# Two weight matrices turned token-major, the residual kept by rows, and the group at each stage boundary run once per half of the tokens

## The chip, the cores and the metric

The kernel runs on one core of one Trainium2 chip. The metric is the device time of one execution in microseconds (us), as the median over several runs. The kernel before takes 2888.52 us (3 runs, 2887.72 to 2889.67).

## The reference

The program computes one step of a two-layer backbone (`DEPTH = 2`) on 256 tokens: 128 context tokens (half 0) and 128 latent tokens (half 1), each half with its own modulation vector. The model width is 2048 and the FFN's hidden width is 8192. Everything is float32. What matters here of each layer:

```python
def _layer(x, cvec, p, attend):
    shift1, scale1, gate1, shift2, scale2, gate2 = _modulation(cvec, p['w_mod'], p['b_mod'])
    h = _rmsnorm(x, p['g_pre_mix']) * (1 + scale1) + shift1
    ...                                    # gMLP and attention branches on h @ w_in
    x = x + gate1 * _rmsnorm(merged @ p['w_out'], p['g_post_mix'])
    h = _rmsnorm(x, p['g_pre_ffn']) * (1 + scale2) + shift2
    f = jnp.square(jax.nn.relu(h @ p['w_ff1'])) @ p['w_ff2']
    x = x + gate2 * _rmsnorm(f, p['g_post_ffn'])
```

So each layer has two stages, mixing and FFN, and between two stages stands a chain that no matmul of the next stage can pass: the sum of squares of the last product over its whole row, the gated residual, the sum of squares of the new residual, and the modulated input `h` of the next stage. There are three such boundaries and an end.

## The kernel before, in words

All weights stream from HBM in tiles of 512 KB, 256 rows by 512 columns. One tile is one **job** (`Job`), and 4 or 8 jobs with the same 512 output columns are one **group** (`Group`, accumulated in PSUM over 8 jobs). The exact float32 product is made from three products of float32r halves: `split` (line 325) makes a high half `wh` on ScalarE (ACT) and a low half `wl` on VectorE (DVE) of every tile, and `mm_half` (line 333) issues the matmuls of one job. There are 928 jobs.

`mm_half` has two forms. With `tok=True` (lines 347 to 349, token-major) the activations are stationary and the weights move: 12 matmuls of 512 columns for a job, and the output has tokens on the partitions. Otherwise (lines 356 to 358, feature-major) the weights are stationary and the 256 tokens move: 24 matmuls of 256 columns for a job, and the output has features on the partitions. `w_out` (64 jobs in both layers), `w_ff1` and `w_ff2` (256 jobs each) are feature-major here, and so is the residual `X`.

The order of all engines' work is the program's order (`tc.manual_schedule`): a list `items` of jobs and callables is walked once. Before each item `advance` issues what it may: a load of a modulation tile while fewer than `MOD_BUFS` (4) are outstanding, a load of a weight tile while fewer than `RAW_BUFS` (6) are, and a split while fewer than `SPLIT_BUFS` (4) split tiles are unused. All loads go out on SP's queue in that order.

The modulation `m = silu(c) @ w_mod` is 384 further tiles ("mods", `one_mod`), in 48 quads of 8. A mod is done on TensorE (PE, `mod_mm`, line 241, for quads in `PE_QUADS`) or on DVE (`mod_dot`, two SCALAR_TENSOR_TENSOR of 1024 elements). Mods are mixed into the stream of jobs: one is issued after a job if a quota (`pace`) asks for it and a count of DVE's cost (`load["dve"]`, written up by each instruction and written down by 2.62 with each job) is below `MOD_LIMIT` (2.0). What must be there at a point is forced by `need(n)`, which issues all mods up to quad n at once. `ENDS` says which quad must be done at the end of each stage: 18, 30, 42, 48.

At a boundary (`boundary`, line 760) the steps are `s1` (root of the mean square, spread over the tokens by PE), `s2_` (residual and its squares, summed by 16 fp32 matmuls of `ones_sum`, line 260, for the two halves' tokens at once), `s3` (second root, first parts of `h`), and then single jobs of the next stage alternate with parts of `h_steps`. `FILLS` puts mods between these steps: quads 18, 19, 30, 31, 42 and 43 are PE mods for that reason. Their loads use up to `X_BUFS` (6) more buffers than the four. At the end, `s1` and `s2_` run alone and send `yT`.

## Time and profile before

| | |
|---|---|
| median of 3 runs | 2888.52 us |
| the profiled execution's own time | 2883.49 us |
| its span, first to last instruction | 2881.7 us |
| mean granted TensorE clock | 0.993 |
| PE busy / DVE busy / ACT busy | 98% / 72% / 46% |
| DMA | 714.63 MB, 248 GB/s mean |

The profile is one execution; its own time stands 5.0 us below the median of the runs. A busy PE is not PE at its peak, since the ends of matmuls are modelled and overlap: what tells PE's pace is the distance between the starts of its instructions. The stages lie at about 0 to 692 us (mixing 0), 717 to 1460 (FFN 0), 1483 to 2099 (mixing 1) and 2122 to 2863 (FFN 1).

### The profile page before, as it was taken

How to read it: one execution, taken by the hardware profiler on the slowest of the kernel's cores; microseconds unless marked ns; L12 is line 12 of the kernel's file. 1: busy time of each engine (PE TensorE's matmuls, PEld its weight loads, DVE VectorE, ACT ScalarE, POOL GpSimd, SP SyncE). 2: the span in 40 equal slices, each digit the busy share in tenths (PEclk: the TensorE clock that was granted, in tenths of full speed). 3: DMA queues.
4: the chain of work that ended last, by engine and by line, in shares of the span. 5: the costliest groups of instructions: out<-in, count | busy, mean ns of one | idle time of the engine just before them, and what ended most of it. 6: DMA issues, size and time to landing. Idle time of an engine off the chain costs nothing.

```text
span 2881.7 us, 50046 instructions
## 1 busy us (share of the span) xinstructions
PE 2821.7 (98%) x20552; PEld 2601.6 (90%) x20552; DVE 2075.3 (72%) x2647; ACT 1336.9 (46%) x1667; POOL 0.7 (0%) x6
## 2 busy tenths in 40 slices
PE   7999999999999999999989999999999999999997
PEld 5788778897999999999969987888979999999997
DVE  4665888888688777777666888898876556556555
ACT  4344554444544434434554445544554444353443
POOL 0000000000000000000000000000000000000000
PEclk9999999999999999999999999999999999999999
DMA  9978877789577777777776687787975566656653
GB/s 358 378 261 306 290 238 252 264 292 338 185 235 262 244 253 238 254 244 246 250 265 237 225 281 249 236 271 264 335 252 191 197 206 207 208 199 217 202 183 108
DMA packets 199046, 714.63 MB, mean 248 GB/s; under 512 B 22304, under 2 KB 24864, under 8 KB 198816
## 3 DMA queue, kind: packets, MB, share of 16 engines
q1 hardware_dynamic: 198816, 711.43, 71.6%
q8 instruction: 161, 2.64, 0.4%
q14 instruction: 69, 0.57, 0.1%
HBM read 705.04 MB, written 6.31 MB: 247 GB/s over the span
## 4 chain that ended last, share of the span: by engine, by line
PE 93%; DVE 3%; ACT 2%; issue 1%; DMA 1%; SPq 0%; ACTq 0%; DVEq 0%
PE mm L356 22%; PE mm L358 22%; PE mm L357 22%; PE mm L347 7%; PE mm L348 7%; PE mm L349 7%; PE aux L241 2%; DVE u L82 2%; PE aux L260 1%; ACT u L82 1%; DVE wl L82 1%; ACT wh L82 1%; DMA mraw<-wm 0%; DVE junk L82 0%; PE aux L545 0%
## 5 line engine op out<-in xcount | busy, mean ns | idle before, releaser
L82 DVE TENSOR_TENSOR wl<-raw,wh 128x1024 fp32r<-128x1024 f32 x928 | 1124.3, 1223 | 573.2 <-ACT wh L82 566.9
L82 ACT ACTIVATE wh<-raw 128x1024 fp32r<-128x1024 f32 x928 | 974.0, 1058 | 1212.3 <-PE mm L357 854.4
L356 PE MATMUL mm<-u,wh 128*128 128x256 f32 x5376 | 1525.2, 284 | 3.4 <-ACT wh L82 3.4
L358 PE MATMUL mm<-u,wl 128*128 128x256 f32 x5376 | 1522.1, 283 | 1.5 <-DVE wl L82 1.5
L357 PE MATMUL mm<-u,wh 128*128 128x256 f32 x5376 | 1522.8, 283 | 0.3
L356 PEld LDWEIGHTS mm<-u,wh 128*128 128x128 f32 x5376 | 1032.5, 192 | 18.2 <-issue 10.9
L358 PEld LDWEIGHTS mm<-u,wl 128*128 128x128 f32 x5376 | 1032.6, 192 | 1.9 <-DVE wl L82 1.9
L357 PEld LDWEIGHTS mm<-u,wh 128*128 128x128 f32 x5376 | 1032.6, 192 | 1.6 <-DVE u L82 1.1
L347 PE MATMUL mm<-wh,u 128*128 128x512 f32 x1024 | 407.0, 397 | 5.1 <-ACT u L82 2.7
L348 PE MATMUL mm<-wl,u 128*128 128x512 f32 x1024 | 400.2, 391 | 0.8 <-DVE wl L82 0.8
L349 PE MATMUL mm<-wh,u 128*128 128x512 f32 x1024 | 400.2, 391 | 0.2 <-DVE u L82 0.2
L82 DVE SCALAR_TENSOR_TENSOR mraw<-mraw,sbc 128x1024 f32<-128x1024 f32 x222 | 272.0, 1225 | 7.7
L82 DVE SCALAR_TENSOR_TENSOR junk<-mraw,sbc 128x1024 bf16<-128x1024 f32 x222 | 270.4, 1218 | 0.0
L347 PEld LDWEIGHTS mm<-wh,u 128*128 128x128 f32 x1024 | 192.9, 188 | 57.4 <-issue 12.8
L349 PEld LDWEIGHTS mm<-wh,u 128*128 128x128 f32 x1024 | 192.9, 188 | 42.4 <-DVE u L82 1.3
L348 PEld LDWEIGHTS mm<-wl,u 128*128 128x128 f32 x1024 | 193.2, 189 | 39.0 <-DVE wl L82 1.1
L82 DVE TENSOR_TENSOR u<-u,u 128x512 fp32r<-128x512 f32 (+3 forms) x139 | 104.2, 769 | 98.0 <-ACT u L82 97.2
L82 ACT ACTIVATE u<-u 128x512 fp32r<-128x512 f32 (+3 forms) x174 | 126.4, 746 | 72.5 <-DVE u L82 65.6
L82 ACT ACTIVATE u<-mm 128x1024 f32<-128x1024 f32 (+1 forms) x95 | 86.7, 925 | 146.5 <-PE mm L358 108.6
L82 DVE TENSOR_TENSOR u<-u,mm 128x1024 f32<-128x1024 f32 (+1 forms) x54 | 63.5, 1180 | 62.3 <-PE mm L358 50.8
L241 PE MATMUL aux<-mraw,csw 128*32 128x512 f32 (+1 forms) x332 | 47.9, 614 | 12.5 <-DMA mraw<-wm 12.4
L82 ACT ACTIVATE u<-u,mv 128x128 f32<-128x128 f32 x114 | 41.5, 431 | 16.1 <-DVE u L82 14.1
(93 smaller groups left out, 723.5 us busy)
## 6 DMA issues: line engine op xcount, KB each, us to landing
raw<-f SPq DMA_DIRECT2D x512, 512.0 KB, 4.3
mraw<-wm SPq DMA_DIRECT2D x297, 512.0 KB, 4.4
raw<-wi SPq DMA_DIRECT2D x288, 512.0 KB, 4.6
u<-wm SPq DMA_DIRECT2D x87, 512.0 KB, 9.3
raw<-wo SPq DMA_DIRECT2D x64, 512.0 KB, 5.0
raw<-pa SPq DMA_DIRECT2D x32, 512.0 KB, 4.7
raw<-pb SPq DMA_DIRECT2D x32, 512.0 KB, 4.4
u<-xT SPq DMA_DIRECT2D x8, 512.0 KB, 7.5
```

What stands on the lines that cost most here:

```text
L82: return fn(out, *a, **k)
L241: nc.tensor.matmul(p[32 * c:32 * c + 32, :128 * nb], csw[:, kt, :], r[:, kt - k0, :], start=kt < 4, stop=kt > 11, skip_group_check=True, t ...
L260: nc.tensor.matmul(o[:, :T], ones, t[:, b, :], start=first and b == 0, stop=last and b == n - 1)
L347: nc.tensor.matmul(o, hh, wh[:, j, :], start=first, stop=False)
L348: nc.tensor.matmul(o, hh, wl[:, j, :], start=False, stop=False)
L349: nc.tensor.matmul(o, lo, wh[:, j, :], start=False, stop=last)
L356: nc.tensor.matmul(o, wh[:, j, s], hh, start=first and b % 2 == 0, stop=False, **kw)
L357: nc.tensor.matmul(o, wh[:, j, s], lo, start=False, stop=False, **kw)
L358: nc.tensor.matmul(o, wl[:, j, s], hh, start=False, stop=last, **kw)
```

## The change

`w_out`, `w_ff2` and the first group of each `w_ff1` become token-major, and the residual `X`, the gate and the output are kept by rows (tokens on the partitions). The last group of each stage and the first group of the next run once per half of the tokens: `lay_halves` issues the eight jobs for half 0 and then the same eight for half 1, with all eight split tiles held (`HELD = 8`). The chain of half 0 (`chain`, twelve steps between `yield`s) is put between the jobs of half 1 of the last group, and goes on between the jobs of half 0 of the next stage's first group, where the chain of half 1 begins. The gate is transposed on PE, written to HBM and read back as rows by eight DMAs (`load_gate`). `FILLS` and the extra load buffers are gone; `need(ENDS[i - 1])` now stands before the last group, and `ENDS` is 20, 34, 44, 48. Four PE quads become DVE quads. One pool of 42 tiles takes the place of four pools.

```diff
-U4_BUFS = 25
-S2_BUFS = 5
+HELD = 8
+BUFS = 42
+S2_BUFS = 6
-ENDS = [18, 30, 42, 48]
-PE_QUADS = set(range(11)) | {18, 19, 30, 31, 42, 43}
+ENDS = [20, 34, 44, 48]
+PE_QUADS = set(range(11)) | {18, 19}
-X_BUFS = 6
-FILLS = [2, 2, 4, 2, 0, 0, 2, 2, 2]
+CHAIN_AT = (0, 1, 3, 4, 5, 6, 7, 8, 9, 10, 11, 12)
...
-    def mm_half(job):
+    def mm_half(job, gs=(0, 1)):
             if G.tok:
-                for g in range(2):
+                for g in gs:
...
-            jobs = gtiles(io["wo"][l, o], Group(8, mg, post_out(o)))
+            jobs = gtiles(io["wo"][l, o], Group(8, mg, post_out(o), True))
...
+    def load_gate(Y):
+        def go():
+            l, m = Y["l"], Y["m"]
+            o = aux()
+            nc.tensor.transpose(o[:32, :128], mv[:, l, m].rearrange("p k g -> p (k g)"), ident)
+            t = s2()[:32, :128]
+            act(t, o[:32, :128], AF.Copy)
+            d = gd[l, m // 3]
+            nc.sync.dma_start(d.rearrange("g (k p) -> k g p", p=128), t)
+            Y["y"] = []
+            for k in range(4):
+                y = v4(u4(), 2)
+                Y["y"].append(y)
+                for g in range(2):
+                    nc.sync.dma_start(y[:, g, :], d[g:g + 1, 512 * k:512 * k + 512].to_broadcast([128, 512]))
+        return go
+
+    def out_stats(Y, src, o, g):
+        act(dump, src, AF.Square, accum_out=Y["st"][g][:, o:o + 1])
+        y = Y["y"][o][:, g, :]
+        tt(y, src, y, op=OP.mult)
...
+        def post_ff1_rows(hid):
+            def turn(t, g):
+                yield
+                o = aux()
+                for b in range(4):
+                    nc.tensor.transpose(o[:, 128 * b:128 * b + 128], t[:, 128 * b:128 * b + 128], ident)
...
-                seq.append(gtiles(io["f2"][l, o, 8 * c:8 * c + 8], Group(8, hid, post_ff2(c, o))))
+                seq.append(gtiles(io["f2"][l, o, 8 * c:8 * c + 8], Group(8, hid, post_ff2(c, o), True)))
...
+    def chain(Y, hs, nxt, spill, g):
+        def rms(st):
+            s = tiny(1)
+            dve.tensor_reduce(s, st, axis=AX.X, op=OP.add)
+            return rms_cols(s)
+        r = rms(Y["st"][g])
+        yield
+        st = tiny(4)
+        for o in range(4):
+            x = X[o][:, g, :]
+            dve.scalar_tensor_tensor(x, Y["y"][o][:, g, :], r, x, op0=OP.mult, op1=OP.add)
+            if nxt is None:
+                nc.sync.dma_start(io["y"][:, o, g], x)
+                continue
+            act(dump, x, AF.Square, accum_out=st[:, o:o + 1])
+            if spill is not None:
+                nc.sync.dma_start(spill[:, o, g], x)
         if nxt is None:
+            return
+        yield
+        r2 = rms(st)
+        yield
...
+        for o in range(4):
+            xr = s2()
+            dve.tensor_scalar(xr, X[o][:, g, :], r2, None, op0=OP.mult)
+            if t is not None:
+                low(o - 1, t)
+            yield
+            if g == 0:
+                hs.extend([pair(), pair()])
+            ps = aux()
+            for b in range(4):
+                nc.tensor.transpose(ps[:, 128 * b:128 * b + 128], xr[:, 128 * b:128 * b + 128], ident)
+            t = v4(s2())
+            for b in range(4):
+                sc, sh = mat(ln, ma, 4 * o + b, g), mat(ln, mb, 4 * o + b, g)
+                src = v4(ps)[:, b, :]
+                if b % 2 == 0:
+                    dve.tensor_scalar(t[:, b, :], src, sc, sh, op0=OP.mult, op1=OP.add)
+                else:
+                    act(t[:, b, :], src, AF.Identity, scale=sc, bias=sh)
+            for e in range(2):
+                act(hs[2 * o + e][:, :, 0, w], t[:, 2 * e:2 * e + 2, :], AF.Copy)
+            yield
+        low(3, t)
...
+    def lay_halves(jobs, nows=None):
+        for g in range(2):
+            for k, j in enumerate(jobs):
+                if nows is not None:
+                    items.append(nows(8 * g + k))
+                items.append((j, (g,), g == 1))
+        loads.extend(jobs)
...
     for i in range(1, 5):
+        seq, Y = seqs[i - 1]
+        items += [need((12, 24, 36, 48)[i - 1]), load_gate(Y)]
+        lay(seq[-LAST[i - 1]:-1])
+        items.insert(len(items) - 8, cap(HELD))
+        items.append(need(ENDS[i - 1]))
...
+        first = (lambda a: lambda p: (lambda: step(0, p - 8, *a)()))(args)
+        lay_halves(seq[-1], first)
         if i == 4:
+            items += [step(1, p, *args) for p in range(2)]
             break
+        def second(p, a=args):
+            def go():
+                step(0, p + 8, *a)()
+                step(1, p, *a)()
+            return go
+        lay_halves(seqs[i][0][0], second)
+        items.append(cap(SPLIT_BUFS))
+        items.append(to_end(ENDS[i], 8 * (24 if i == 2 else 30), i))
...
-            if P["nm"] < len(mloads) and (P["mlive"] < MOD_BUFS or P["xlive"] < (START_BUFS if P["nm"] < 64 else P["xb"])):
+            if P["nm"] < len(mloads) and P["mlive"] < MOD_BUFS + (START_BUFS if P["nm"] < 64 else 0):
...
-            if P["nl"] < len(loads) and P["live"] < RAW_BUFS and loads[P["nl"]].after <= P["nm"]:
+            if P["nl"] < len(loads) and P["live"] < RAW_BUFS - (P["cap"] == HELD) * 2 and loads[P["nl"]].after <= P["nm"]:
```

## Rows read from the trace of the kernel before

**Rows 1.** The page: busy time by engine (its share of the span, and instructions), and the chain of waits that ended last, by engine.

```profile
PE 2821.7 (98%) x20552; PEld 2601.6 (90%) x20552; DVE 2075.3 (72%) x2647; ACT 1336.9 (46%) x1667; POOL 0.7 (0%) x6
...
PE 93%; DVE 3%; ACT 2%; issue 1%; DMA 1%; SPq 0%; ACTq 0%; DVEq 0%
```

**Rows 2.** PE's timeline in FFN 0, the first and the last of 29 feature-major matmuls in a row with nothing between them (start us, duration us, engine, line, operation).

```profile
899.57 0.28 PE L357 MATMUL mm<-u,wh 128*128 128x256 f32 x1
...
902.93 0.28 PE L358 MATMUL mm<-u,wl 128*128 128x256 f32 x1
```

**Rows 3.** PE's timeline in mixing 0, the first and the last of 29 token-major matmuls in a row with nothing between them.

```profile
519.61 0.39 PE L348 MATMUL mm<-wl,u 128*128 128x512 f32 x1
...
525.96 0.39 PE L349 MATMUL mm<-wh,u 128*128 128x512 f32 x1
```

**Rows 4.** The jobs' matmuls (tile `mm`) in three stretches, each from the last matmul of a stage to where the next stage runs evenly: the stretch and its length in us, PE busy us (and count), granted clock, DMA share, GB/s. In the second, 66 of the 258 are feature-major and 192 token-major.

```profile
692.20:760.00 67.80, 40.23 (x313) 0.92 0.68 242
1459.90:1540.00 80.10, 53.91 (x258) 0.96 0.71 254
2099.50:2180.00 80.50, 55.64 (x455) 0.98 0.63 225
```

**Rows 5.** PE's timeline at boundary 1: the last matmul of mixing 0, the last four 128x128 transposes ahead of the next stage (in brackets an idle time and what ended it), and that stage's first matmul.

```profile
692.13 0.28 PE L358 MATMUL mm<-u,wl 128*128 128x256 f32 x1
...
716.95 0.66 PE L223 MATMUL aux<-ident,s 128*128 128x128 f32 x4 [0.16 <-ACT s L82]
717.36 0.36 PE L356 MATMUL mm<-u,wh 128*128 128x256 f32 x1
```

**Rows 6.** The timeline at the end: the last matmul, the next work on DVE, the last work on DVE.

```profile
2862.98 0.28 PE L358 MATMUL mm<-u,wl 128*128 128x256 f32 x1
2863.30 1.28 DVE L82 TENSOR_TENSOR u<-u,mm 128x512 f32<-128x512 f32 x2 [9.32 <-PE mm L358]
...
2877.93 0.69 DVE L82 TENSOR_TENSOR u<-u,u 128x512 f32<-128x512 f32 x1
```

**Rows 7.** Groups of instructions by line, shapes kept apart, costliest first: operation, out<-in, shapes, count | busy us, mean ns of one | idle before, what ended it.

```profile
L82 ACT ACTIVATE wh<-raw 128x1024 fp32r<-128x1024 f32 x928 | 974.0, 1058 | 1212.3 <-PE mm L357 854.4 <-PE mm L349 305.2 <-DMA raw<-wi 19.1
...
L82 ACT ACTIVATE u<-u,mv 128x128 f32<-128x128 f32 x114 | 41.5, 431 | 16.1 <-DVE u L82 14.1 <-DVE mv L82 1.8
...
L82 DVE TENSOR_SCALAR u<-u,mv 128x128 f32<-128x128 f32 x78 | 23.2, 343 | 1.1
...
L82 ACT ACTIVATE u<-u 128x512 f32<-128x512 f32 x16 | 9.7, 628 | 25.9 <-DVE u L82 25.9
...
L82 DVE TENSOR_TENSOR u<-u,u 128x256 fp32r<-128x256 f32 x14 | 5.9, 423 | 0.1
...
L82 ACT ACTIVATE u<-u 128x256 fp32r<-128x256 f32 x14 | 5.8, 416 | 8.0 <-DVE u L82 7.2
...
L82 DVE TENSOR_TENSOR u<-u,mm 128x512 f32<-128x512 f32 x4 | 2.6, 684 | 10.0 <-PE mm L358 10.0
...
L82 ACT ACTIVATE tiny<-aux,epsb 128x2 f32<-128x2 f32 x5 | 1.3, 258 | 5.7 <-PE aux L894 4.8 <-PE aux L774 0.9
```

**Rows 8.** DVE's timeline after boundary 2: two scalings of 128 columns, and four low halves of splits back to back.

```profile
1481.44 0.60 DVE L82 TENSOR_SCALAR u<-u,mv 128x128 f32<-128x128 f32 x2
...
1494.40 4.63 DVE L82 TENSOR_TENSOR wl<-raw,wh 128x1024 fp32r<-128x1024 f32 x4 [0.25 <-ACT wh L82]
```

**Rows 9.** ACT's timeline in mixing 0, some 70 us ahead of boundary 1: the load of the table for the square root and the next instruction.

```profile
621.26 1.28 ACT L82 ACT_TABLE_LOAD   x1
622.56 0.20 ACT L82 ACTIVATE tiny<-epsb 128x1 f32<-128x1 f32 x1
```

**Rows 10.** PE's timeline after boundary 2, around a wait.

```profile
1494.42 0.49 PE L347 MATMUL mm<-wh,u 128*128 128x512 f32 x1 [2.30 <-ACT wh L82]
1495.68 0.79 PE L348 MATMUL mm<-wl,u 128*128 128x512 f32 x1 [0.76 <-DVE wl L82]
1496.27 0.63 PE L349 MATMUL mm<-wh,u 128*128 128x512 f32 x1
1496.70 0.63 PE L347 MATMUL mm<-wh,u 128*128 128x512 f32 x1
```

**Rows 11.** DVE's timeline at the end of mixing 0: the fold that follows the third of the four groups of `w_out`, then the first half of the first and of the last of the five mods that come after it.

```profile
671.05 1.15 DVE L82 TENSOR_TENSOR u<-u 128x512 f32<-128x512 f32 x2
...
675.75 1.22 DVE L82 SCALAR_TENSOR_TENSOR junk<-u,sbc 128x1024 bf16<-128x1024 f32 x1
...
695.68 1.22 DVE L82 SCALAR_TENSOR_TENSOR junk<-u,sbc 128x1024 bf16<-128x1024 f32 x1
```

**Rows 12.** DMA issues of modulation tiles: count, size, median us from issue to landing.

```profile
mraw<-wm SPq DMA_DIRECT2D x297, 512.0 KB, 4.4
```

**Rows 13.** All engines in three stretches (start-up, token-major in mixing 0, FFN 0): the stretch and its length, busy us (and count) of PE, PEld, DVE, ACT and POOL, granted clock, DMA share, GB/s.

```profile
80.00:120.00 40.00, 39.84 (x281) 31.57 (x284) 24.54 (x33) 15.16 (x19) 0.00 (x0) 1.00 1.03 409
480.00:600.00 120.00, 119.86 (x543) 98.83 (x543) 106.97 (x138) 51.88 (x53) 0.00 (x0) 1.00 0.81 271
1080.00:1200.00 120.00, 120.00 (x1002) 120.00 (x1002) 90.84 (x116) 56.47 (x58) 0.00 (x0) 1.00 0.74 245
```

**Rows 14.** DVE's timeline at the end of mixing 1: the first half of the first and of the last of the three mods that come after the third group of `w_out`.

```profile
2083.09 1.22 DVE L82 SCALAR_TENSOR_TENSOR junk<-u,sbc 128x1024 bf16<-128x1024 f32 x1
...
2093.26 1.22 DVE L82 SCALAR_TENSOR_TENSOR junk<-u,sbc 128x1024 bf16<-128x1024 f32 x1
```

More of the change, by code (lines that the diff above doesn't have):

```diff
@@ L255, in hi_lo @@
         tt(hl[:, :, 1, :], t, f(hl[:, :, 0, :]), op=OP.subtract)
-    def ones_sum(o, t, first, last):
-        n = t.shape[1]
-        for b in range(n):
-            nc.tensor.matmul(o[:, :T], ones, t[:, b, :], start=first and b == 0, stop=last and b == n - 1)
     def rms_cols(src):
-        r = tiny(2)
+        r = tiny(src.shape[1])
         act(r, src, AF.Sqrt, bias=epsb, scale=1.0 / D)
@@ L864, in need, with cap, step @@
         return go
-    def hold():
-        P["hold"] = True
-    def extra(n):
+    def cap(n):
         def go():
-            P["xb"] = n
+            P["cap"] = n
+        return go
+    chains = [[], []]
+    def step(g, n, *args):
+        def go():
+            if n == 0:
+                chains[g].append(chain(*args, g))
+            if n in CHAIN_AT and chains[g]:
+                pump(chains[g])
         return go
@@ L975, in body @@
         if i == 4:
-            items += boundary(Y, None, None)
+            items += [step(1, p, *args) for p in range(2)]
             break
-        nxt = (i // 2, 1, 0) if i % 2 == 0 else (i // 2, 4, 3)
-        items.append(need(ENDS[i - 1]))
-        chain, steps = boundary(Y, hs[i], nxt, xd if i == 2 else None)
-        items += chain
-        items.append(extra(0))
-        items.append(to_end(ENDS[i], 8 * (26 if i == 2 else 32), i))
-        first = seqs[i][0][0]
-        for j, n in zip(first, H_STEPS[1:]):
-            lay([[j]])
-            items.append(steps(n))
@@ L1041, in one_mod, with ease @@
         P["md"] += 1
[L1042 removed]
+        P["mlive"] -= 1
     def quota():
         return P["m0"] + P["rate"] * (P["t"] - P["t0"])
[L1047 removed]
+    def ease(n):
         for k in load:
[L1049 removed]
+            load[k] = max(0.0, load[k] - 2.62 * n)
     for it in items:
[L1052 removed]
         if callable(it):
+            if not P["free"]:
+                advance()
             it()
@@ L1059, in body @@
         else:
+            advance()
+            job, gs, last = it
             pump(bgm)
@@ L1062, in body @@
                 pump(bg)
-            mm_half(it)
-            P["sp"] -= 1
-            P["t"] += 1
+            mm_half(job, gs)
+            P["sp"] -= last
+            P["t"] += len(gs) / 2 if job.group.tok else 1
             spread_s()
@@ L1073, in body @@
                     one_mod()
-            ease()
-            G = it.group
-            if G.part and it.kh in (0, 1, 3, 5, 7):
-                if it.kh == 0:
+            ease(len(gs) / 2)
+            G = job.group
+            if G.part and job.kh in (0, 1, 3, 5, 7):
+                if job.kh == 0:
                     G.acc = u4()
```

262 lines of the change are left out of this document (84 added, 178 removed).

## The prediction, made before the changed kernel was run

> **What bounds the kernel now.** I read the page first: PE is busy for 98% of the span and stands on 93% of the chain that ended last [rows 1]. So only PE's own pace and the places where it waits count. Pace is the distance between starts: 28 steps of a feature-major matmul take 3.36 us, 0.120 each [rows 2], 28 steps of a token-major one 6.35 us, 0.2268 each [rows 3]. A feature-major job is 24 x 0.120 = 2.88 us, a token-major one 12 x 0.2268 = 2.72 us.
>
> Then the three boundaries: a stretch's length less its matmuls at these paces is what the boundary costs. 67.8 - 313 x 0.120 = 30.2; 80.1 - 66 x 0.120 - 192 x 0.2268 = 28.6; 80.5 - 455 x 0.120 = 25.9 [rows 4]: 84.7 in all, the fill-in mods included. At boundary 1, 25.2 of the 30.2 pass before the first new matmul [rows 5]. The end costs 2881.7 - 2863.0 = 18.7 us after the last matmul [rows 6].
>
> **Part 1, token-major.** 64 + 256 jobs of `w_out` and `w_ff2` and 16 of the first FFN groups: 336 x 0.158 = **53.2 us less**. PE's pace there is even, so this part is the surest.
>
> **Part 2, the end.** Half 0's chain runs under half 1's last matmuls. For half 1 remain: add from PSUM (starts 0.32 after the matmul, takes 0.68), square (0.63, and about 0.2 for its sum), three small steps (about 0.9), four row updates of 0.68 [rows 6, 7]: 5.5 us; from DVE's last work to the end it was 3.1 [rows 6] and stays. 8.6 in place of 18.7: **10.1 less**.
>
> **Part 3, the chain between the halves.** The old 84.7 goes: its sixteen summing matmuls, its spreads, its fill-ins. What comes instead I count from the end of half 0 of an FFN's last group (0), with durations of rows 7, a split's low half at 4.63 / 4 = 1.16 and a scaling at 0.26 to 0.30 [rows 8]. PE goes on with half 1, 6 x 0.2268 = 1.36 a half job, and comes to the first four transposes (step 5) at 6.8. They need the first scaled rows, and on DVE, in the program's order, stand before these: add, statistics, root, reciprocal (to 2.7), four updates (5.4) whose squares on ACT end at 6.6, two splits whose high halves queue on ACT behind the squares (10.0), second root (10.8), third split (12.8), then the scaled rows: 13.4. **PE waits 6.6.** Each next set stands behind the one before: scalings, two splits, a subtraction of low halves; the sets are ready at 18.7, 26.1, 33.4, while PE has only two half jobs (2.7) to run between two sets. It waits 2.1, 4.2 and 4.1, and 1.2 for half 1's first set. Sum 18.2, and eight sets of four transposes at 0.41 (716.95 to 717.36, rows 5) make 3.3: 21.5 a boundary, **64.5 for three**. Bounds: 4 if the splits run ahead, 30 if each handover between ACT and DVE costs more.
>
> At the two mixing boundaries the table for the square root, which was loaded 70 us ahead, is now loaded inside the chain: 2 x 1.3 [rows 9] = **2.6**. The Trainium skill (ScalarE: Activation LUTs, What ACT_TABLE_LOAD costs) counts a drain of 1.38 us with every load, 2.66 in all, which speaks against this change; by it the sum is 2.8 higher. The trace doesn't show that drain here: the next activation starts 1.30 after the load did [rows 9].
>
> The scaling of 512 columns is not in the trace; I take 0.6, below the 0.68 of a two-operand step of that size [rows 7]. The Trainium skill (VectorE: DVE Perf Modes, The perf-mode tier table) gives a float32 `tensor_scalar` between SBUF tiles twice the rate of `tensor_tensor`. By that it is about 0.4, and the sum some 2.4 lower.
>
> After a wait of 2.3 us and one of 0.8, PE's matmuls stood 0.43 apart and not 0.2268: the granted clock was at its lower level, 1.2 GHz of 2.4 [rows 10]. The new waits are shorter and spread; I take 2 a boundary, **6**, since slow matmuls between two waits mostly eat the next wait.
>
> **Part 4, mods that must be there.** `need` now stands before the last group, and for mixing 0 it asks for 20 quads. In the trace five DVE mods come after the third group of `w_out` [rows 11]. Four more held splits (4 x 1.155 on the meter, against 1.46 written off a job) push two more behind: 7 DVE mods, and then all 16 PE mods of quads 18 and 19, which the old kernel did as fill-ins. PE cannot pass these 16, and only four loads are ahead. The 19 others follow as buffers come free: the first behind DVE mods (2.45 apart), the rest at 512 KB a time. Each takes 4.4 to land [rows 12] and, at the busiest rate seen, 409 GB/s, 1.28 of transfer [rows 13]. With two spare buffers, a load issued as each mod ends, I come to 36 us; 19 x 1.28 = 24 is the floor, 40 the other bound. I take **34**. In mixing 1 three mods are left at that point [rows 14], with the two more pushed behind 5, all on DVE: 5 x 2.45 = 12 against 10.9 of PE work in half 0, so half 0's chain, behind them on DVE, starts late by some **5** with its hand-overs.
>
> **Small parts.** Four sets of transposes for the FFNs' first groups and four for the gates: **3**. FFN 0 gets 112 DVE mods for 80. DVE's need for a job there is a split 1.16, 112 / (240 x 0.92) = 0.507 mods x 2.45, and 0.15 of adds: 2.55 against PE's 2.72; while it catches up after the chain the meter lets through 0.567 mods, 2.70. In mixing 0 DVE was busy 107 of 120 us and PE lost nothing [rows 13]. I take **3**. The gate's store and eight loads (2 MB) go on SP's queue, which waits for the store: raw tiles six jobs ahead (16 us) cover it; without that cover each boundary loses up to 10. The spill is eight DMAs for four, the output eight for five; behind them only loads with that same cover, so nothing.
>
> **Sum:** -53.2 - 10.1 - 84.7 + 64.5 + 2.6 + 6 + 34 + 5 + 3 + 3 = -29.9. The profiled execution took 2883.5, so 2853.6; the median of the runs stands 5.0 above it, so I forecast **2859**. Its own range is 2835 to 2885.
>
> **Rivals.** (a) *The halves hide the chain.* If the splits don't delay DVE's chain, only the 3.3 of transposes and a little are left at a boundary, 4 in place of 21.5, and the forced loads go at their floor: 2859 - 52 - 10 = 2797. For it: ACT was busy 56 of 120 us in an FFN [rows 13], so there is room. Against: in-order queues, and 16 splits (19 us of DVE) fall into the same three halves as two chains of about 12 each. (b) *Faster matmuls, but the boundaries eat it.* Chain 30 a boundary, forced loads 40: 2859 + 25 + 6 = 2890, no change. (c) *DVE becomes the bound in FFN 0, slower.* It decides when a job's DVE work passes 2.72; at 2.55 to 2.70 it is near. If in-order waits between ACT and DVE cost 0.2 us in each of the 240 jobs, that is 48: 2907. For it: 32 more mods there, 78 us of DVE. Against: PE lost nothing at 89% DVE.
>
> **How the numbers follow.** Forecast 0.45, (a) 0.20, (b) 0.12, (c) 0.23. About 0.2% (5.8 us) can be told from no change. The forecast's cases are faster, all but a few hundredths, and so is (a): faster 0.63; (b) and the edge: same 0.13; slower 0.24. The range reaches down to nearly all of (a) and up to (c): 2800 to 2905.
>
> **What would show it.** Token-major matmuls 0.2268 apart in FFN 0's second matrix, 2.72 a job; else part 1 is wrong. Between mixing 0's third and fourth group of `w_out`, 16 PE mods with waits for their loads, 30 us or more; if that stretch is below 15, part 4 is wrong. At each boundary, PE waits for DVE's scaled rows ahead of the transposes, the first the longest. About 8.6 us after the last matmul. In FFN 0, PE waits for `wl` would show (c); boundaries of under 8 us would show (a).

## The result and the profile after

The changed kernel takes **2869.23 us** (median of 4 runs, 2868.43 to 2871.44) against 2888.66 (4 runs): ratio 0.9934, interval 0.9917 to 0.9951, 19.4 us less where 29.9 were forecast. The profiled execution took 2869.5 us, its span is 2867.7: 14.0 shorter than the span before.

The page: busy time by engine, and the chain of waits that ended last, as in [rows 1]. PE has 4186 instructions and 61 us of busy time less, yet its share of the span fell from 98% to 96%: it waits more than before.

```profile
PE 2761.1 (96%) x16366; PEld 2386.6 (83%) x16366; DVE 2114.4 (74%) x2782; ACT 1288.7 (45%) x1654; POOL 0.7 (0%) x6
...
PE 91%; DVE 3%; ACT 3%; DMA 1%; issue 1%; SPq 0%; DVEq 0%; ACTq 0%
```

All engines in 40 us of FFN 0's second matrix, columns as in [rows 13]. PE is never without work although DVE is busy for 38.3 of the 40 us. From 790 to 1430 us PE's time over its paces is 0.8 us in all.

```profile
1040.00:1080.00 40.00, 40.00 (x178) 33.15 (x177) 38.32 (x51) 15.80 (x16) 0.00 (x0) 1.00 0.79 287
```

The end, to hold against [rows 6]: the first and the last of twenty matmuls in a row (19 steps in 4.30 us, 0.226 each, as in [rows 3]), then half 1's add, row updates and stores. From the last matmul to the end of the span (2867.7) are 8.6 us.

```profile
2854.84 0.39 PE L319 MATMUL mm<-wl,u 128*128 128x512 f32 x1
...
2859.14 0.39 PE L320 MATMUL mm<-wh,u 128*128 128x512 f32 x1
2859.57 0.69 DVE L76 TENSOR_TENSOR u<-u,mm 128x512 f32<-128x512 f32 x1 [6.97 <-PE mm L320]
...
2861.82 2.74 DVE L76 SCALAR_TENSOR_TENSOR u<-u,tiny,u 128x512 f32<-128x512 f32 x4
2862.60 2.32 SPq L774 DMA_DIRECT2D y<-u  x4
```

The forced mods at the end of mixing 0, PE's timeline: the last matmul of `w_out`'s third group, the first and the last of the 16 PE mods (four matmuls each), the fourth group's first matmul. The fourth group begins 38.8 us after the third ended, of which the first 12.6 are one wait.

```profile
666.73 0.39 PE L320 MATMUL mm<-wh,u 128*128 128x512 f32 x1
679.67 1.92 PE L234 MATMUL aux<-mraw,csw 128*32 128x512 f32 x4 [12.55 <-DMA mraw<-wm]
...
703.37 1.05 PE L234 MATMUL aux<-mraw,csw 128*32 128x512 f32 x4 [0.24 <-DMA mraw<-wm]
704.35 1.42 PE L216 MATMUL aux<-ident,s 128*128 128x128 f32 x8
705.53 0.48 PE L318 MATMUL mm<-wh,u 128*128 128x512 f32 x1
```

The jobs' matmuls around the three boundaries, columns as in [rows 4]. The first two rows together hold 193 token-major and 94 feature-major matmuls, the third 296 token-major ones, the fourth 239 and 51.

```profile
666.95:705.50 38.55, 0.17 (x1) 0.78 0.87 326
705.50:790.00 84.50, 61.96 (x286) 0.94 0.39 137
1430.00:1530.00 100.00, 77.04 (x296) 0.90 0.50 172
2080.00:2170.00 90.00, 68.26 (x290) 0.92 0.48 166
```

By the paces of [rows 2, 3] as in the prediction, the boundaries cost 68.0 (forced mods included), 32.9 and 29.7: **130.6 us**, where 84.7 stood before and 112.1 were forecast.

Boundary 2 of the changed kernel, PE's timeline, only the instructions that PE waited for by more than 0.3 us: the start of half 1 of the last FFN group (1464.30), the four sets of transposes for half 0, the start of half 1 of the next group (1511.35), and one set of half 1.

```profile
1464.30 0.50 PE L318 MATMUL mm<-wh,u 128*128 128x512 f32 x1 [0.78 <-DVE u L76]
...
1476.04 1.12 PE L803 MATMUL aux<-ident,s 128*128 128x128 f32 x4 [4.66 <-DVE s L76]
...
1482.31 0.66 PE L803 MATMUL aux<-ident,s 128*128 128x128 f32 x4 [0.75 <-DVE s L76]
...
1490.39 0.77 PE L803 MATMUL aux<-ident,s 128*128 128x128 f32 x4 [4.67 <-DVE s L76]
...
1497.96 1.11 PE L803 MATMUL aux<-ident,s 128*128 128x128 f32 x4 [2.56 <-DVE s L76]
...
1511.35 0.79 PE L318 MATMUL mm<-wh,u 128*128 128x512 f32 x1 [3.06 <-ACT u L76]
...
1520.13 0.66 PE L803 MATMUL aux<-ident,s 128*128 128x128 f32 x4 [2.38 <-DVE s L76]
```

Those seven waits sum to 18.9 us; 18.2 were forecast. But what follows a wait is slow. The same timeline behind the wait that ended at 1476.04: matmuls 0.43 apart at first, 0.24 from 1480.69 on.

```profile
1477.38 0.63 PE L319 MATMUL mm<-wl,u 128*128 128x512 f32 x1
1477.81 0.63 PE L320 MATMUL mm<-wh,u 128*128 128x512 f32 x1
...
1480.69 0.40 PE L318 MATMUL mm<-wh,u 128*128 128x512 f32 x1
1480.93 0.39 PE L319 MATMUL mm<-wl,u 128*128 128x512 f32 x1
```

And that stretch as a whole (length, all of PE's instructions, granted clock, DMA share, GB/s): a mean of 0.59, most of it at 1.2 GHz of 2.4.

```profile
1476.04:1481.50 5.46, 5.46 (x16) 0.59 0.63 222
```

To split a boundary I walked all starts of PE between the forced mods and the even run. What a step from one job matmul to the next takes over its pace, less a wait that the timeline names, is **slow clock**; steps out of other instructions are **transposes**; named waits over 0.3 us are **idle**. In "slow clock" 1.2 to 1.3 us of each boundary are not clock: around each wait some 0.16 us pass that neither the pace nor the wait counts.

| changed kernel, us | idle | transposes | slow clock | sum |
|---|---|---|---|---|
| boundary 1 | 19.1 | 4.0 | 6.8 | 29.9 |
| boundary 2 | 18.9 | 4.2 | 10.1 | 33.2 |
| boundary 3 | 18.6 | 3.8 | 7.6 | 30.0 |
| three boundaries | 56.6 | 12.0 | 24.5 | 93.1 |
| forecast (waits 18.2 x 3, tables 2.6, late chain 5; 3.3 x 3; 6) | 62.2 | 9.9 | 6 | 78.1 |

### The profile page after: what moved, and what is told of

It reads as the page before. It is cut to its first block, busy times and chain, and to the rows that moved or that the text cites. A ratio compares the mean times of both kernels' runs of the same rounds, so it can differ in the third digit from the quotient of the medians.

```text
span 2867.7 us, 41916 instructions
## 1 busy us (share of the span) xinstructions
PE 2761.1 (96%) x16366; PEld 2386.6 (83%) x16366; DVE 2114.4 (74%) x2782; ACT 1288.7 (45%) x1654; POOL 0.7 (0%) x6
## 4 chain that ended last, share of the span: by engine, by line
PE 91%; DVE 3%; ACT 3%; DMA 1%; issue 1%; SPq 0%; DVEq 0%; ACTq 0%
PE mm L318 18%; PE mm L320 18%; PE mm L319 18%; PE mm L327 11%; PE mm L328 11%; PE mm L329 11%; PE aux L234 2%; ACT wh L76 1%; DVE u L76 1%; DVE wl L76 1%; DMA mraw<-wm 1%; DVE s L76 1%; ACT s L76 1%; ACT u L76 1%; PE aux L803 0%
## 5 line engine op out<-in xcount | busy, mean ns | idle before, releaser
L318 PE MATMUL mm<-wh,u 128*128 128x512 f32 x2368 | 940.9, 397 | 13.6 <-ACT u L76 5.6
L320 PE MATMUL mm<-wh,u 128*128 128x512 f32 x2368 | 929.4, 392 | 1.5 <-DVE u L76 1.5
L319 PE MATMUL mm<-wl,u 128*128 128x512 f32 x2368 | 930.0, 393 | 0.4 <-DVE wl L76 0.4
L327 PE MATMUL mm<-u,wh 128*128 128x256 f32 x2688 | 763.8, 284 | 0.0
L329 PE MATMUL mm<-u,wl 128*128 128x256 f32 x2688 | 761.1, 283 | 0.0
L328 PE MATMUL mm<-u,wh 128*128 128x256 f32 x2688 | 761.1, 283 | 0.0
L318 PEld LDWEIGHTS mm<-wh,u 128*128 128x128 f32 x2368 | 449.7, 190 | 119.5 <-issue 7.7
L320 PEld LDWEIGHTS mm<-wh,u 128*128 128x128 f32 x2368 | 449.2, 190 | 98.1 <-DVE u L76 2.9
L327 PEld LDWEIGHTS mm<-u,wh 128*128 128x128 f32 x2688 | 516.1, 192 | 13.8 <-issue 10.9
L319 PEld LDWEIGHTS mm<-wl,u 128*128 128x128 f32 x2368 | 449.6, 190 | 90.8 <-DVE wl L76 0.8
L328 PEld LDWEIGHTS mm<-u,wh 128*128 128x128 f32 x2688 | 516.1, 192 | 0.4
L329 PEld LDWEIGHTS mm<-u,wl 128*128 128x128 f32 x2688 | 516.1, 192 | 0.0
L76 DVE SCALAR_TENSOR_TENSOR mraw<-mraw,sbc 128x1024 f32<-128x1024 f32 x280 | 343.0, 1225 | 9.7
L76 DVE SCALAR_TENSOR_TENSOR junk<-mraw,sbc 128x1024 bf16<-128x1024 f32 x280 | 340.9, 1217 | 0.0
L76 ACT ACTIVATE u<-u 128x512 fp32r<-128x512 f32 (+3 forms) x116 | 84.2, 753 | 33.2 <-DVE u L76 27.3
```

The lines of the kernel that those rows point to most:

```text
L76: return fn(out, *a, **k)
L318: nc.tensor.matmul(o, hh, wh[:, j, :], start=first, stop=False)
L319: nc.tensor.matmul(o, hh, wl[:, j, :], start=False, stop=False)
L320: nc.tensor.matmul(o, lo, wh[:, j, :], start=False, stop=last)
L327: nc.tensor.matmul(o, wh[:, j, s], hh, start=first and b % 2 == 0, stop=False, **kw)
L328: nc.tensor.matmul(o, wh[:, j, s], lo, start=False, stop=False, **kw)
```

## The experiments

Each run is set against the kernel before by its ratio, since the medians of before moved between 2883.9 and 2888.6 from one set of runs to the next; "against the changed kernel" is the difference of the two ratios times 2888.7 (the text on experiments 2 to 4 gives differences of medians, up to 0.9 us away from it). Boundary cost is what the stretches above come to when treated in the same way (boundary 3 of experiments 9 and 12, which comes sooner, from 2065 us). Experiment 1 is built on the kernel before, the others on the changed kernel.

| run | ratio, interval | against the changed kernel | boundary cost 1 / 2 / 3 |
|---|---|---|---|
| changed kernel | 0.9934 (0.9917 to 0.9951) | | 68.0 / 32.9 / 29.7 |
| 1 token-major alone | 0.9820 (0.9806 to 0.9835) | -32.9 | |
| 2 two more PE quads | 0.9912 (0.9897 to 0.9927) | -6.4 | 48.4 / 31.1 / 30.2 |
| 3 scalings on ACT | 0.9882 (0.9868 to 0.9897) | -15.0 | 61.7 / 28.1 / 24.8 |
| 4 PSUM tile per half | 0.9901 (0.9885 to 0.9918) | -9.5 | 65.6 / 28.3 / 28.2 |
| 5 no halves | 0.9917 (0.9901 to 0.9934) | -4.9 | 58.9 / 30.8 / 30.9 |
| 6 = 3 + 4 | 0.9862 (0.9848 to 0.9877) | -20.8 | 62.1 / 23.3 / 23.2 |
| 7 = 3 + 4 + 2 | 0.9849 (0.9834 to 0.9864) | -24.6 | 42.6 / 23.3 / 23.3 |
| 8 scalings on DVE | 0.9908 (0.9893 to 0.9923) | -7.5 | 64.2 / 29.5 / 26.2 |
| 9 = 6 + late hold | 0.9830 (0.9816 to 0.9845) | -30.0 | 50.7 / 24.4 / 23.7 |
| 10 = 5 + 3 | 0.9877 (0.9861 to 0.9894) | -16.5 | 53.6 / 27.2 / 27.6 |
| 11 = 9 + 2 | 0.9846 (0.9832 to 0.9861) | -25.4 | 37.1 / 25.6 / 23.3 |
| 12 = 9 + late splits | 0.9806 (0.9791 to 0.9821) | -37.0 | 47.2 / 20.3 / 20.8 |

**1. Token-major alone,** in the kernel before.

```diff
-            jobs = gtiles(io["wo"][l, o], Group(8, mg, post_out(o)))
+            jobs = gtiles(io["wo"][l, o], Group(8, mg, post_out(o), True))
-                seq.append(gtiles(io["f2"][l, o, 8 * c:8 * c + 8], Group(8, hid, post_ff2(c, o))))
+                seq.append(gtiles(io["f2"][l, o, 8 * c:8 * c + 8], Group(8, hid, post_ff2(c, o), True)))
```

> The kernel before, with the output projection and the second FFN matrix issued token-major and nothing else changed (the products then lie the other way round in the residual, so the outputs are not the reference's; every instruction's shape and place is as in the kernel before but for these 320 jobs). Theory (the gain of the change is PE's pace): 320 x 0.158 = 50.6 us less than before, 2838, so the rest of the change costs about 31. Rival (the gain comes from the boundaries, and a job's pace is set by DVE's splits or the loads): no more than 15 us less, 2874 or above.

The steps at the boundaries are left as they were and take rows for features. 2835.94 us against 2888.61: 52.7 less, where 50.6 were expected. So the pace carries the gain, and all that comes with it (rows, halves, forced mods, less the shorter end) costs some 33 us. What follows looks for those.

**2. Two more quads on PE,** so that they are done in the stream and not forced.

```diff
-PE_QUADS = set(range(11)) | {18, 19}
+PE_QUADS = set(range(11)) | {16, 17, 18, 19}
```

> The changed kernel with quads 16 and 17 on PE as well, so that DVE has 16 mods fewer before the end of mixing 0 and none has to be forced there. Theory (37 us of PE's time between the third and the fourth group of the output projection are waits for the loads of forced mods): that stretch shrinks to under 5, the 32 PE mods cost 32 x 0.465 = 15 in the stream, 22 us less than the changed kernel, about 2847. Rival (the stretch is only where DVE's backlog shows, and returns elsewhere): at most 7 us less, 2862 or above.

2861.97 us: 7.3 less than the changed kernel, not 22. The cost at boundary 1 fell by 19.6, but 24 of the now 32 PE mods stand in the stream of jobs, 18 of them before 667 us. Experiments 9 and 11, which differ by this edit alone, show what those 18 cost: from 480 to 667 us PE's time over its paces rose from 4.4 to 20.1 us, 0.87 a mod where the theory took 0.465. The stretch with the eight that are still forced is 14.6 us (685.88 to 700.44) in place of 38.8; with 24 x 0.87 = 20.9 in the stream that is 35.5. So the rival's number was right. What comes back is PE's own work on 16 more mods.

**3. All four scalings of a set on ACT.** In the changed kernel they alternate. DVE's timeline at boundary 2, and ACT's below it, show the four scalings of one set: each starts when the other engine's has ended, though they write different columns of `s`. They also read one PSUM tile, `aux`; the last section comes back to that.

```profile
1477.20 0.41 DVE L76 TENSOR_SCALAR s<-aux,mv 128x128 f32<-128x128 f32 x1
1478.14 0.41 DVE L76 TENSOR_SCALAR s<-aux,mv 128x128 f32<-128x128 f32 x1 [0.53 <-ACT s L76]
```

```profile
1477.65 0.46 ACT L76 ACTIVATE s<-aux,mv 128x128 f32<-128x128 f32 x1 [2.37 <-DVE s L76]
1478.58 0.46 ACT L76 ACTIVATE s<-aux,mv 128x128 f32<-128x128 f32 x1 [0.48 <-DVE s L76]
```

```diff
-                if b % 2 == 0:
-                    dve.tensor_scalar(t[:, b, :], src, sc, sh, op0=OP.mult, op1=OP.add)
-                else:
-                    act(t[:, b, :], src, AF.Identity, scale=sc, bias=sh)
+                act(t[:, b, :], src, AF.Identity, scale=sc, bias=sh)
```

> The changed kernel with all four scalings of a transposed set on ACT, not two on DVE and two on ACT in turn. Theory A (the four wait for one another across the engines, 1.9 us a set, and DVE's queue stands behind them): each set is ready about 1 us sooner, 2 to 4 us less a boundary, 6 to 12 less in all, 2857 to 2863. Theory B (the splits between the chain's steps set when a set is ready, and ACT has to do them too): no change within 3 us, or slower.

2854.36 us, 15 less, more than expected. The boundaries fall by 6.3, 4.8 and 4.9. In a row on ACT the four take 1.51 us (in the trace of experiment 6) in place of 1.8:

```profile
1470.81 1.51 ACT L76 ACTIVATE s<-aux,mv 128x128 f32<-128x128 f32 x4 [1.92 <-PE aux L803]
```

**4. A PSUM tile for each half.** In the changed kernel both halves of a group write one tile (in different columns), and the second half's first matmul waits for the readers of the first: 1464.30 and 1511.35 above.

```diff
-                if last:
-                    G.ps = None
+                G.ps = None
```

> The changed kernel with a PSUM tile of its own for each half of a halved group, so that half 1's first matmul need not wait until half 0's results have been read. The six waits there come to about 11 us in the changed kernel's trace. Theory: the three in the last groups are given back at the next transposes, which wait for DVE anyway; those in the first groups stay: 4 to 6 us less, about 2864. Rival (all of them are on the path): 11 less, 2858; other rival (all given back): no change.

2859.75 us, 9.5 less. The waits of halves are gone; the first transposes of half 0 now wait 5.7 to 6.2 us in place of 4.2 to 4.7, since PE arrives at them sooner. That is the 6.6 of the prediction, which had no wait of halves in it.

**5. No halves.** The last group of a stage and the first of the next run whole, and the two chains go in a row between them.

```diff
-        items.insert(len(items) - 8, cap(HELD))
...
-        lay_halves(seq[-1], first)
+        lay([seq[-1]])
+        items += [step(g, p, *args) for p in range(2 if i == 4 else 13) for g in range(2)]
...
-        lay_halves(seqs[i][0][0], second)
+        lay([seqs[i][0][0]])
```

> The changed kernel with the last group of each layer and the first of the next run whole again, for both token halves at once; the two chains then run in a row between the groups with nothing of TensorE's between them but background transposes. All else (token-major matrices, row residual, chain by rows) stays. Theory (the halves hide the chain, though not fully): at each of the three inner boundaries TensorE waits for two chains of 13 steps, shared on DVE and ACT, that is at least one chain's length (four sets of some 5 us and two reductions, 25 to 32 us) less the waits that the changed kernel already shows there (14 to 20 us), so +10 to +15 us a boundary, and the end after the last matmul grows from 8.6 us to some 14 to 18: 2869 + 30 to 45 + 5 to 9 = 2905 to 2923, middle 2912. Rival (the halves hide nothing, what they hide they give back in waits of their own): within 5 us of 2869.

Ratio 0.9917, **no slower than with halves**: the theory's middle was off by some 47 us, 12 of them by the forced stretch (below). The chain now stands bare, four sets of eight transposes each behind its wait, and then the next stage's first matmul:

```profile
1476.49 1.97 PE L803 MATMUL aux<-ident,s 128*128 128x128 f32 x8 [12.09 <-DVE s L76]
1481.33 2.18 PE L803 MATMUL aux<-ident,s 128*128 128x128 f32 x8 [2.88 <-DVE s L76]
1486.71 2.15 PE L803 MATMUL aux<-ident,s 128*128 128x128 f32 x8 [3.19 <-ACT s L76]
1491.99 2.15 PE L803 MATMUL aux<-ident,s 128*128 128x128 f32 x8 [3.13 <-ACT s L76]
1493.80 0.78 PE L318 MATMUL mm<-wh,u 128*128 128x512 f32 x1
```

At boundary 2 that is 21.3 us idle, 8.1 in transposes and 1.7 of slow clock; with halves it is 18.9, 4.2 and 10.1. So two chains in a row are hardly longer than one taken in pieces (the second runs in the gaps of the first), and the job matmuls meet the lower clock once and not several times. The 8.1 in transposes are at the lower clock too, 3.9 more than with halves. Boundaries 2 and 3 are the same within 2 us each way. The end is 12.9 us after the last matmul in place of 8.6, and the forced stretch is 26.5 us (666.48 to 693.00) in place of 38.8. These 12.3 us are not the halves' own doing: the edit also drops `cap(HELD)` ahead of the forced mods, which experiment 9 moves while the halves stay. Leaving them aside, the kernel with halves is some 7 us ahead.

**6. Edits 3 and 4 together.**

> Both single edits together: the four scalings of a set all on ACT, and a PSUM tile of its own for each half of a group. Theory (the two losses lie at different places of the boundary, and part of the second is already gone with the first): the trace with scalings on ACT still shows waits of halves of 1.3, 2.7, 1.3 and 2.0 us = 7.3 us; of the 11 us of such waits the single edit won 9.5, the same share of 7.3 is 6.3, so 2854.4 - 6.3 = 2848. Rival 1 (independent, both add up): 2869.2 - 14.9 - 9.5 = 2845. Rival 2 (the same wait: what one wins the other has won already): 2854, no change against scalings on ACT.

Ratio 0.9862: 20.8 less, next to the theory (21.3). Full addition (24.5) lies at the edge of the interval. Boundaries 2 and 3 now cost 23.3 and 23.2.

**7. And two more quads on PE.**

> The two edits of the kernel with ACT scalings and own PSUM tiles, and two more modulation groups on TensorE (PE_QUADS with 16 and 17), so that less of the work forced at the end of mixing 0 is left. Theory (the forced stretch lies before the boundary and is independent of it): a further -7.3 us as alone, some 2841. Rival (the stretch of forced jobs had covered the chain's beginning or the splits of boundary 1, so without it the boundary waits longer): no gain against the kernel with the two edits, 2848.

Ratio 0.9849, 3.8 less than experiment 6 with overlapping intervals: between the theory and the rival, not told apart.

**8. All four scalings on DVE.**

```diff
-                if b % 2 == 0:
-                    dve.tensor_scalar(t[:, b, :], src, sc, sh, op0=OP.mult, op1=OP.add)
-                else:
-                    act(t[:, b, :], src, AF.Identity, scale=sc, bias=sh)
+                dve.tensor_scalar(t[:, b, :], src, sc, sh, op0=OP.mult, op1=OP.add)
```

> The changed kernel with all four scalings of a set on DVE instead of in turns with ACT. It tells why ACT alone gained 15 us. Theory A (the turns between the engines cost: each scaling waits 0.48 to 0.53 us for the one before on the other engine): four scalings of 0.41 us in a row on DVE are done 0.3 to 0.5 us sooner than the four in turns (1.9 us), over 24 sets 7 to 12 us: 2857 to 2862. Rival B (DVE is the engine that the sets wait for, held by the splits' subtractions of 1.22 us; ACT alone gained by taking work off it): two more scalings a set on DVE, 0.7 us x 24 = up to 17 us later: 2869 to 2886.

Ratio 0.9908: 7.5 less. So the turns cost by themselves: theory A holds, B doesn't. That ACT wins another 7.5 fits with the copies that read the scaled tile next and also run on ACT; this was not tried by itself.

**9. The hold set late,** on experiment 6. `cap(HELD)` stood eight jobs ahead of the forced mods.

```diff
-        items.insert(len(items) - 8, cap(HELD))
         items.append(need(ENDS[i - 1]))
+        items.append(cap(HELD))
```

> The kernel with ACT scalings and own PSUM tiles (ratio 0.9862 to before), and the raised number of held split weights set after the forced modulation jobs at the end of a layer instead of eight jobs before them. Theory (with the early setting four more weight tiles are split and as many more raw tiles are requested ahead of the modulation tiles on SP's queue, so that TensorE's first forced job at mixing 0's end waits 12.5 us for its tile; without halves that wait was 4.1 us and the stretch of forced jobs 26 us instead of 38): the stretch shrinks by 8 to 12 us, ratio 0.982 to 0.984, some 2837 us against 2889. Rival (the splits only move: done after the forced jobs, some 5 us of them on ACT and DVE stand in front of the last group's first half or in the chain's way at all three boundaries): the stretch shrinks, but the boundaries grow by 3 to 5 us each, ratio 0.985 to 0.988.

Ratio 0.9830: 9.2 less than experiment 6. DVE's timeline, first the changed kernel, then this one, each with the first half of the first and of the last mod after the third group of `w_out`: seven mods at 2.41 apart, and five.

```profile
671.40 1.22 DVE L76 SCALAR_TENSOR_TENSOR junk<-mraw,sbc 128x1024 bf16<-128x1024 f32 x1
...
685.88 1.22 DVE L76 SCALAR_TENSOR_TENSOR junk<-mraw,sbc 128x1024 bf16<-128x1024 f32 x1
```

```profile
670.69 1.22 DVE L76 SCALAR_TENSOR_TENSOR junk<-mraw,sbc 128x1024 bf16<-128x1024 f32 x1
...
680.34 1.22 DVE L76 SCALAR_TENSOR_TENSOR junk<-mraw,sbc 128x1024 bf16<-128x1024 f32 x1
```

PE's timeline of this kernel, as above for the changed one: the first wait is 3.8 us and not 12.6, and the stretch is 27.9 us.

```profile
666.01 0.39 PE L320 MATMUL mm<-wh,u 128*128 128x512 f32 x1
670.21 4.89 PE L234 MATMUL aux<-mraw,csw 128*32 128x512 f32 x16 [3.81 <-DMA mraw<-wm]
...
693.87 0.47 PE L318 MATMUL mm<-wh,u 128*128 128x512 f32 x1
```

SP's timeline of the changed kernel, two loads of mods with only loads of `w_out` between them: for 19.7 us none goes out. DVE does nine low halves in a row there (10.3 us from 648.51) and no mod, and the program asks for a further mod's tile only when one is done.

```profile
639.07 0.33 SPq L1007 DMA_DIRECT2D mraw<-wm  x1
...
658.76 0.33 SPq L1007 DMA_DIRECT2D mraw<-wm  x1
```

Between 640 and 666 us the changed kernel issues two loads of mods, this one eight. So four early splits cost 11 us there: they hold back two DVE mods, and with them the loads of the PE mods. The weight tiles that the expectation saw ahead on SP's queue are the smaller part: from 640 to 668 us eleven in place of nine. The splits did not come back as a loss: boundaries 2 and 3 are within 1.1 us of experiment 6.

**10. No halves, scalings on ACT** (edits 5 and 3).

> The kernel without halves (ratio 0.9917), with all scalings on ACT. It tells what halves are worth once their two hindrances are gone: without halves against with halves and both edits (0.9862, whose first boundary still holds 12 us more of forced jobs). Theory (the turns between the engines cost without halves too, but less, since there the two halves' sets overlap and one engine's wait is filled by the other half's work): boundary overhead falls from 31 to 28 or 29 us, ratio 0.9895 to 0.991; so the halves with both edits gain some 5 to 8 us a boundary (23.3 against 28 to 31), and the worth of halving is real, but was eaten in the kernel as changed. Rival (ACT alone wins as much here: 5 us and more a boundary, ratio 0.987 and below): then the halves hide nothing even mended.

Ratio 0.9877; boundaries 27.2 and 27.6, between theory and rival. Against experiment 9, which differs in the halves and the two PSUM tiles, halves are worth 3 to 4 us a boundary and the shorter end (8.6 for 12.9): 0.9877 - 0.9830, 13.6 us in all. They pay once their own hindrances are gone.

**11. Experiment 9 with two more quads on PE.**

> All four edits: ACT scalings, own PSUM tiles, the held number set after the forced jobs, and two more modulation groups on TensorE. Theory (the two edits on the forced jobs work on the same stretch: with the two groups moved, the stretch was 13 to 14 us already and its waits for tiles 4 us): the two together win little over the better one: within 4 us of the kernel without the two groups moved. Rival (independent): a further 3 to 5 us as with the two edits alone.

Ratio 0.9846: 4.6 us slower than experiment 9, just outside the theory's 4 us, and against the rival. The intervals overlap, but each of its four runs is slower than each of experiment 9's. The 13.6 us that boundary 1 loses are less than the 15.7 that the mods cost ahead of it (experiment 2).

**12. No splits in front of the chain,** on experiment 9. DVE's timeline of experiment 9 at boundary 2, from the row updates to the first scaled rows: three low halves of splits stand between, and the first two wait for their high halves on ACT.

```profile
1448.61 2.74 DVE L76 SCALAR_TENSOR_TENSOR u<-u,tiny,u 128x512 f32<-128x512 f32 x4
1453.42 2.36 DVE L76 TENSOR_TENSOR wl<-raw,wh 128x1024 fp32r<-128x1024 f32 x2 [2.08 <-ACT wh L76]
...
1457.16 1.22 DVE L76 TENSOR_TENSOR wl<-raw,wh 128x1024 fp32r<-128x1024 f32 x1 [0.78 <-ACT wh L76]
1458.30 0.48 DVE L76 TENSOR_SCALAR s<-u,tiny 128x512 f32<-128x512 f32 x1
```

The edit allows no split in the first four jobs of half 1, then two a job (`late` is set to 1 when half 0's chain begins). Two more lines, not shown, let as many more weight tiles be loaded meanwhile as are not split, so that their requests stay where they were:

```diff
-            if P["ns"] < P["nl"] and P["sp"] < P["cap"]:
+            if P["ns"] < P["nl"] and P["sp"] < P["cap"] and P["quota"] > 0:
                 split(loads[P["ns"]])
+                P["quota"] -= P["late"] > 0
...
+            if P["late"]:
+                P["quota"] = 0 if P["late"] < 5 else 2
+                P["late"] = (P["late"] + 1) % 9
             advance()
```

> The kernel with ACT scalings, own PSUM tiles and the late hold (ratio 0.983), and in half 1 of a layer's last group no weight tile is split until half 0's chain has scaled its first rows by the norm (four jobs later); then up to two splits a job. Raw tiles are requested as before. In the trace without this edit the chain of boundary 2 stands from 1452.35 to 1458.30 us behind four splits: two on ACT and DVE before the sum of the norm (1455.70), and one subtraction of 1.22 us before the scaling of the first rows (1458.30); without them the chain would need 0.2 + 0.5 + 0.3 us there. Theory (these splits set the first wait of each boundary, 5.7 to 6.2 us): the first wait shrinks by 4 to 5 us at each of three boundaries, 12 to 15 us in all, of which the splits that now come later (four of 1.05 us on ACT, beside the scalings) give back up to half: ratio 0.978 to 0.981, 2823 to 2832 us against 2886. Rival (the splits are needed anyway before the next group's half 0 and only move the wait to its first jobs and the later sets): boundary overhead stays at 23 to 25 us, ratio 0.983.

2829.53 us, ratio **0.9806, the fastest version**: 37 us below the changed kernel. From the end of the updates to the scaled rows DVE's chain now takes 1.9 us instead of 7:

```profile
1445.29 2.74 DVE L76 SCALAR_TENSOR_TENSOR u<-u,tiny,u 128x512 f32<-128x512 f32 x4
...
1449.88 0.49 DVE L76 TENSOR_SCALAR s<-u,tiny 128x512 f32<-128x512 f32 x1
```

and the wait ahead of the first transposes fell from 5.67 to 0.57 us. The next sets give part of it back; PE's timeline of both at the second set, first experiment 9, then this one:

```profile
1464.76 0.66 PE L803 MATMUL aux<-ident,s 128*128 128x128 f32 x4 [0.86 <-DVE s L76]
```

```profile
1457.33 0.66 PE L803 MATMUL aux<-ident,s 128*128 128x128 f32 x4 [3.52 <-DVE s L76]
```

Boundary costs of 20.3 and 20.8 in place of 24.4 and 23.7: of about 5 us that the first wait loses, some 3 to 4 are kept. At boundary 2 they are hardly kept as idle time: split as above it has 14.8 us idle, 3.2 in transposes and 2.7 of slow clock, against 15.7, 3.5 and 5.6 in experiment 9.

## Why the prediction was right, and what was mis-sized

The time lies in the range that was given, 10 us above the forecast.

**Part 1 was right.** The pace is that of [rows 3], PE ran without a gap at 38.3 of 40 us of DVE, and token-major alone won 52.7 us by experiment 1, against 50.6 for its 320 jobs.

**Part 2 was right:** 8.6 forecast, 8.6 measured. Experiment 5 shows what of it halving brings: 12.9 without.

**Part 4 was right in its mechanism:** seven DVE mods and 16 PE mods, the first held back by loads behind DVE mods. The price was 38.8 us, not 34 (40 was the upper bound); experiment 9 shows that two of the seven are 11 us of it. The late chain in mixing 1 (5) is not to be seen: boundary 3's idle time is that of the others. DVE had one mod left after the third group there (2094.78 to 2097.3), not five, and then stood idle for 4.5 us until half 0's add.

**Part 3: the waits were right in sum, by luck.** 18.2 forecast, 18.6 to 19.1 idle. The first wait came as worked out: splits stand in the chain's way, which experiment 12 shows by moving them, and it is 6.6 forecast against 5.7 to 6.2 where halves have a PSUM tile each. But two causes were missing, the readers of a PSUM tile that the halves share (experiment 4, 9.5 us) and scalings that wait for one another (experiments 3 and 8, 15.0 and 7.5 us). At boundary 2 the two waits of halves (3.8) made up in the sum for a first wait that was 1.9 shorter and later ones that were 1.2 shorter. The later sets did not come sooner than forecast: they are 6.3, 8.1 and 7.6 apart, for 5.3, 7.4 and 7.3. PE's slower matmuls between them took the time that would have been a wait.

A scaling of 512 columns took 0.48 us (1458.30 above), where I took 0.6. The 0.4 that the prediction worked out by the Trainium skill (VectorE: DVE Perf Modes, The perf-mode tier table) was nearer.

The table load at boundary 1 now lies in the chain, as ACT's timeline shows. The next activation starts 1.29 us after it, as in [rows 9]. The drain that the Trainium skill adds to a load (ScalarE: Activation LUTs, What ACT_TABLE_LOAD costs) is not seen here either.

```profile
717.48 1.28 ACT L76 ACT_TABLE_LOAD   x1
718.77 0.29 ACT L76 ACTIVATE tiny<-tiny,epsb 128x1 f32<-128x1 f32 x1
```

**The step that failed is the list of what the chain waits for:** it had neither of the two causes. Experiment 6 takes both away, and then boundaries 2 and 3 cost 23.3 and 23.2, and boundary 1 24.3 without its forced stretch. The prediction's terms (21.5, 2 for the clock, 1.3 for a table at boundaries 1 and 3) give 23.5, 24.8 and 24.8. The two causes are 20.8 us of the kernel's time, the forced mods came out 4.8 over, and the late chain's 5 did not come: 20.6, against the 18.5 by which the boundaries passed the forecast (130.6 for 112.1). Less the 3 for FFN 0, where PE lost nothing, that is the miss against the profile (2869.5 for 2853.6). Against the medians the miss is 10, since the 5.0 that I added for the distance of the median from the profiled execution does not hold after: there the two stand within 0.3 us.

**The clock is where the excess shows; that it is the cause is not shown.** I took 2 us a boundary, "since slow matmuls between two waits mostly eat the next wait". By the table it is 6.8 to 10.1, 24.5 in all, 18.5 over, and idle time is 56.6 for 62.2. But the two kinds can't be priced apart, since a slow matmul ahead of a wait that ends on DVE makes this wait shorter, as the prediction said: in experiment 6 boundary 2 has 5.3 of slow clock and 14.9 idle, 3.3 over its 2 and 3.3 under its 18.2. How much there is of it depends on how the waits lie. With one long wait and short ones close behind (experiment 5) job matmuls lose 1.7 us at boundary 2, and transposes 3.9 more than with halves; with seven waits spread over 56 us job matmuls lose 10.1. Nor does it go by the sum of the waits: at boundary 2 experiment 12 has half of experiment 9's at nearly the same idle time. What it costs by itself no run isolates.

**The rivals.** (a) was wrong: no chain is hidden, the smallest boundary that four edits reached is 20 us. (b) was nearest of the three: a boundary of 30 to 33 us and forced mods of 38.8 are close to its 30 and 40. But its 30 stood beside 13.6 for tables, clock and a late chain, which the 30 to 33 already hold; with these, its boundaries come to 143.6, 13 over, and the 5.0 and the 3 make the rest of the 21 us by which 2890 is too high. (c) was wrong: DVE at 38.3 of 40 us holds nobody up.

**What the halves do** was not asked by the prediction and should have been: taken out, the time is the same or lower, and they are ahead only by some 7 us when the forced stretch, which the same edit shortens, is left aside. I priced the chain with halves, and never the chain without them.

Open: why scalings on ACT win more than the end of the turns explains, and what the slow clock costs by itself.

## What to carry to other kernels

Before a chain is cut into halves to hide it, price it whole: two chains in a row overlap each other, and halving here was worth 13.6 us once its own hindrances were gone (experiments 9 and 10). Where an order is written out by hand, look for work on the same queues that is not the chain's (splits here) and move it behind the chain's next hand-over, and see that two halves share no PSUM tile whose readers the second has to wait for. Where steps of a chain read one PSUM tile, try them on one engine (experiments 3 and 8). A forced batch is priced by what stands in front of its loads, so nothing that can wait belongs ahead of it.

## What the runs showed of the hardware

After the wait of 4.66 us PE ran at the lower of its two clock levels, 1.2 GHz, until 1480.4 (granted clock 0.50 from 1476.0), while it had work without a pause; behind the 0.75 us wait at 1482.31 it did not (1.00 from 1482.3 to 1485.7). Behind the next wait, 4.67 us, it was at the lower level again for most of 1490.4 to 1494.3 (mean 0.56), though the clock granted during that wait was 1.00. In experiment 5, with a wait of some 3 us ahead of each set, eight transposes take 2.15 us each time, where eight in the changed kernel at 704.35 took 1.42; the granted clock is 0.50 from 1476 to 1494. Its mean granted clock over the whole run, waits included, is 0.982, against 0.988 with halves and 0.994 in experiment 12.

Two engines that only read one PSUM tile take turns too. At the end of `w_out`'s third group ACT squares a half of `mm` and DVE multiplies the same half, into tiles of their own; DVE waits for ACT's first square, and ACT's second square, of other columns, waits for DVE's product:

```profile
667.87 0.69 DVE L76 TENSOR_TENSOR u<-mm,u 128x512 f32<-128x512 f32 x1 [0.21 <-ACT dump L76]
668.60 0.60 ACT L76 ACTIVATE dump<-mm 128x512 bf16<-128x512 f32 x1 [0.76 <-DVE u L76]
```

At boundary 2 the same square and product read a tile in SBUF, and both start at 1454.36. So for the turns of the four scalings it is enough that they read one PSUM tile; whether the shared tile that they write would do the same by itself, no run here tells. A matmul into one half of a PSUM tile whose other half is still read waits as well (1464.30 and 1511.35). Whether the chip or the program's own tracking of tiles asks for these waits, the traces don't tell.
